# Another sequence for the dense jobs of the attention stage, and one set of rotation tiles

## The chip, the cores and the metric

The kernel runs on one core of a Trainium2 chip. The metric is the device time of one execution in microseconds (us). The sequences of TensorE (PE), VectorE (DVE), ScalarE (ACT), GpSimd (POOL) and SyncE (SP) run beside each other, each in its own order, and wait for each other through semaphores. All transfers between memory and the core are issued by SP here, one after the other.

## What is computed

One layer of an encoder over 1024 tokens of width 1024: a gated feed-forward block, a mixing block and a second gated feed-forward block, each with a residual. The change lies in the mixing block:

```python
proj = u @ w_in            # columns: qa, ka, va, xm, o_pre, ga, gb
ya = diff_attention(rope(qa), rope(ka), va)   # 8 heads, two score maps each, block-causal
yb = mlstm_branch(xm, o_pre)                  # 4 heads, conv, chunkwise scan
merged = sigmoid(ga) * (ya @ w_proj_a) + sigmoid(gb) * (yb @ w_proj_b)
h = h + gt2 * (merged @ w_out)
```

`rope` turns each pair (a, b) into (a cos - b sin, a sin + b cos).

## The kernel before

All matrix products are made of three float32r products of high and low parts (`mm3`), so each weight tile is fetched (512 KB, `wr`), cast on ACT into a high part (`wh`) and subtracted on DVE into a low part (`wl`). Two raw buffers (`raw`) and four pairs of high and low parts serve all of them.

The mixing block has two stages with chains of dependent small steps: the mLSTM (`stage_mlstm`) and the attention (`stage_attn`). The gaps that these leave on TensorE are filled with dense jobs, generators that emit a few matmuls at each step (`chunk` takes the next step of the first job in `self.jobs`). There are four kinds.

- `job_qk` (q, one for each head): four halves of 24 matmuls of 512 columns. The first two products are copied by ACT into the tiles `qa0` and `qa1` (one buffer each); the other two are each turned with one of these in `rotate`, which takes eight DVE steps and three ACT copies, writes the rotation tiles `ro` and stores four tiles of 256 KB to memory (`qkh`, `qkl`). The attention stage loads a head's keys and queries from there.
- `job_v` (v, one for two heads): eight tiles of 24 matmuls of 256 columns, each split by ACT and DVE, stored in pairs (`vh`, `vl`).
- `job_g` (g): gate columns, one weight unit and two halves of 24 matmuls for each tile of 128 columns.
- `job_b`: products of the mLSTM output, at the end of the list.

The order of the jobs is a string in `tile_block`: one q, four v, three q, then gates and q in turn. The planner's own times are 21.8 us of TensorE for a q, 21.7 for a v, 10.9 for a g of one tile and 5.45 for a b.

In the mLSTM stage a job is taken whenever the due time of the next mLSTM item lies ahead (`paced`); the order on ACT, DVE and SP is then left to the scheduler of the framework. The attention stage is laid out by a planner of the kernel itself, `Flow`. It simulates TensorE, ACT and DVE with a list of costs, and writes the instructions of all engines out in the order in which they come up in that model. A chain yields steps: "A" and "D" are operations of ACT and DVE with a cost, "P" matmuls, "X" a transfer, "take" and "give" a token that stands for a buffer, "need" and "set" a flag, "wait" a delay that stands for a transfer. When no matmul of the attention is ready, the planner calls `chunk`. The tokens are `raw`, `dn` (two PSUM banks for dense jobs), `rb` and `rot` (rotation), `qa0`, `qa1`, and those of the attention. A weight fetch is given 7 us (`lead`), the last store of a rotation 6.0 us. Jobs are begun up to three ahead, as long as they have no more than four weight units together (`begin_jobs`); a job begun outside the planner has its weights loaded at once, and a q then only the first of two.

Of the kernel before, what the change touches and what calls it, by code (L numbers as in the profile page):

```python
# [54 lines left out]
class Flow:  # L55
# [71 lines left out]
    def run(self):  # L127
        while self.live:
            while self.heap and self.heap[0][0] <= self.now:
                t, _, what = heapq.heappop(self.heap)  # L130
                if not isinstance(what, tuple):
                    self.advance(t, what)
                elif what[1] == "P":
                    self.pe.append(what)
                else:
                    gen, eng, cost, fn = what
                    fn()
                    self.free[eng] = max(self.free[eng], t) + cost
                    self.push(self.free[eng] + self.LAT, gen)
            if self.pe:  # L140
                gen, _, cost, fn = self.pe.pop(0)
                fn()
                self.now += cost
                self.push(self.now + self.LAT, gen)
                continue
            c = self.chunk()
            if c:
                self.now += c
            elif self.heap:
                self.now = max(self.now, self.heap[0][0])  # L150
            else:
                assert not self.live

class Net:
# [901 lines left out]
    def job_v(self, hp):  # L1056
# [10 lines left out]
        def keep(tt):  # L1067
            if tt % 2:
                for x, d in zip(vo, self.vd[hp]):
                    nc.sync.dma_start(out=d[:, :, tt - 1:tt + 1], in_=x)  # L1070

        for tt in range(8):
# [28 lines left out]
    def job_qk(self, hd):  # L1101
# [9 lines left out]
        def first(ps, n):  # L1111
            ab.append([None, [("give", f"qa{n}")] if self.flow else []])
            return [("take", f"qa{n}")] * len(ab[n][1]) + [("A", 0.6, lambda: keep(ps, n))]

        for i in range(2):
            while not w[i][2]:
                yield 0.0
            for n in range(NH):
                yield from self.proj_half(w[i], "qp", n, lambda ps, n=n: first(ps, n) if i == 0
                                          else self.rotate(hd, n, *ab[n], ps))  # L1120
                if len(w) == 1:
                    w.append(self.unit_ahead(self.a["win"][2 * hd + 1]))

    def rotate(self, hd, n, a, done, ps):
        nc, v, ns = self.nc, self.nc.vector, slice(n * NW, n * NW + NW)
# [7 lines left out]
        def to_b():  # L1133
            t["b"] = self.t512()
            nc.scalar.copy(t["b"], ps)

        def to_x():
            for c in "xyw":
                t[c] = self.rope.tile([P, NW], F32, name=self.nm("ro"), tag="ro", bufs=6)
            v.tensor_mul(t["x"], a, cos)  # L1140

# [3 lines left out]
                 ("D", 0.69, lambda: v.tensor_sub(t["x"], t["x"], t["y"])),  # L1145
                 ("D", 0.69, lambda: v.tensor_mul(a, a, sin)),
                 ("A", 0.62, lambda: nc.scalar.copy(t["y"].bitcast(F32R), t["x"])),
                 ("D", 0.69, lambda: v.tensor_mul(t["b"], t["b"], cos)),
                 ("D", 0.69, lambda: v.tensor_add(a, a, t["b"])),
                 ("D", 0.69, lambda: v.tensor_sub(t["x"].bitcast(F32R), t["x"], t["y"])),  # L1150
                 ("X", lambda: store(t["x"], t["y"], 0)),
                 ("A", 0.62, lambda: nc.scalar.copy(t["w"].bitcast(F32R), a)),
                 ("D", 0.69, lambda: v.tensor_sub(a.bitcast(F32R), a, t["w"])),
                 ("X", lambda: (store(a, t["w"], 1), self.turned(hd, n)))]
        if self.flow is None:
            return [x for x in steps if len(x) > 2 or x[0] == "X"]
        return [("take", "rb")] + steps[:8] + [("give", "rb")] + steps[8:] + [("wait", 6.0), ("give", "rot")] + done

    def turned(self, hd, n):

        self.heads_in.add(("qk in", hd, n))
        if self.flow is not None:
            self.flow.set(("qk in", hd, n))

# [27 lines left out]
    def load_y(self, n, src):  # L1192
        nc = self.nc
        ns = slice(n * NW, n * NW + NW)
        if n not in self.y:
            self.y[n] = [[self.u_tile(c, k, n) for c in "hl"] for k in range(KT)]
        done = []
        for k in range(KT):
# [4 lines left out]
            else:  # L1203
                def chain(k=k, hi=hi, lo=lo):
                    yield "wait", 5.0 + 0.7 * k
                    yield "A", 0.62, lambda: nc.scalar.copy(hi, lo.bitcast(F32))
                    yield "D", 0.69, lambda: nc.vector.tensor_sub(lo, lo.bitcast(F32), hi.bitcast(F32))
                    if k == KT - 1:
                        done.append(1)
# [3 lines left out]
    def job_b(self, n, m):  # L1213
# [4 lines left out]
        while not self.loaded[n]:  # L1218
# [4 lines left out]
        ps, free = yield from self.bank("ab")  # L1223
        evict = (("D", 0.7, lambda: nc.vector.tensor_mul(t, t, ps)), *free,
                 ("X", lambda: nc.sync.dma_start(out=self.bd[m][:, ns], in_=t)))

        for k in range(KT):
            ks = slice(k * P, k * P + P)
            if k == 4:
                self.defer(0.5, ("A", 0.63, lambda: nc.scalar.activation(t, t, AF.Exp, scale=-1.0)))  # L1230
            self.mm3(ps, (w[0][:, ks], w[1][:, ks]), [x for x in self.y[n][k]], k == 0, k == KT - 1)
# [21 lines left out]
    def chunk(self):  # L1253

        while self.jobs:
            self.begin_job(0) if self.flow is None else self.begin_jobs()
# [229 lines left out]
    def stage_attn(self, dense):  # L1486
        nc, tc = self.nc, self.tc
        nlam, gcol = self.lam[:, 2:3], self.lam[:, 3:4]
        with tc.tile_pool(name="a1", bufs=1) as a1, tc.tile_pool(name="a2", bufs=2) as a2, \
# [5 lines left out]
            qs, kh, kl = (a1.tile([P, 2, T], F32R, name=self.nm(c), tag=c) for c in ("Q", "Kh", "Kl"))  # L1495
            flow = Flow(lambda: self.chunk() if len(self.jobs) > KT or ("scored", 7, 3) in flow.flags else 0.0,
                        {"raw": 2, "dn": 2, "rb": 1, "rot": 2, "qa0": 1, "qa1": 1, "sc": 2, "pt": 1, "po": 1, "ah": 2, "p0": self.p0, "p1": 2, "osb": 1})

# [37 lines left out]
            def score(hd, j, i, c, a):  # L1536
# [45 lines left out]
                if (i, c) == (1, 1):  # L1582
                    yield "set", ("scored", hd, j)
                yield "D", 0.27 + 1.04e-3 * W, top
                yield "take", f"p{c}"
# [130 lines left out]
            for x in self.heads_in:  # L1716
                flow.set(x)
            self.begin_jobs()
            with tc.manual_schedule(engines={PE, ACT, DVE, SP}):
                self.flow = flow  # L1720
                flow.run()
                self.flow = None
# [45 lines left out]
def tile_block(ctx, tc, aps, dbg=()):  # L1768
# [57 lines left out]
    with ExitStack() as net.outer:  # L1826
        with ExitStack() as gst:
            net.stage_in(gst)
            net.set_lnexp(net.last_sig)
            order = "qvvvvqqqggqggqggqggqggggggg"  # L1830
            src = {"q": [[net.job_qk(hd), 2, None] for hd in range(8)], "v": [[net.job_v(hp), 2, None] for hp in range(4)],
                   "g": [[net.job_g(s, *j), len(j), None] for s, j in [(1, (j,)) for j in range(KT)]
                         + [(0, (j,)) for j in range(KT - 2)] + [(0, (KT - 2, KT - 1))]]}
            net.jobs = [src[c].pop(0) for c in order] + [[net.job_b(n, m), 1, None] for n in range(NH) for m in range(KT)]
            net.y, net.loaded, net.heads_in = {}, {}, set()
            net.left = 4 * 21.7 + 8 * 21.8 + 16 * 10.9 + 16 * 5.45
# [83 lines left out]
```

## Time and profile before

| | us |
|---|---|
| median of 3 runs | 2676.37 |
| their range | 2676.04 to 2682.2 |
| the profiled execution | 2680.27 |
| its span, first to last instruction | 2678.6 |

The profile is of one execution. Its page gives the busy time of each engine; the trace behind it can be asked for stretches of time, for waits and what ended them, for the chain of work that ended last, and for a list of instructions in order. All times within it are counted from the start of the span. The granted clock is a share of the full 2.4 GHz; 0.50 is the lower level, 1.2 GHz, and a figure between is a mean over the stretch. The mixing block's mLSTM stage lies between about 884 and 1203 us, the attention stage between 1203 and about 1840 us.

### The profile page before, as it was taken

The numbers are of one execution on the slowest core, as the hardware profiler recorded it, in microseconds if no ns is written. First come the engines' busy times: TensorE is split into PE (matmuls) and PEld (weight loads), VectorE is DVE, ScalarE is ACT, GpSimd is POOL, SyncE is SP. The second block draws the span as 40 slices with busy tenths as digits, with TensorE's granted clock in tenths as the row PEclk, the third lists the DMA queues.
The fourth block names the chain that finished last, engine by engine and source line by source line (L and its number), as shares of the span: only waits on it lengthen the run. The fifth ranks groups of instructions, "written<-read, shape, count | busy, mean of one in ns | idle before, by whom it ended". The sixth has DMA issues, their size and how long they took to land.

```text
span 2678.6 us, 35281 instructions
## 1 busy us (share of the span) xinstructions
PE 2590.4 (97%) x12704; PEld 2162.5 (81%) x12704; DVE 1789.2 (67%) x3214; ACT 1269.8 (47%) x2374; POOL 22.5 (1%) x85
## 2 busy tenths in 40 slices
PE   6999999999999999998899999999999999999998
PEld 4888888778878789996688888787888888888886
DVE  8977677778786456545666665574557766666967
ACT  6433333446444356653466664664345433334443
POOL 0000000000000000000000000000000000000000
PEclk8999999999999999998899999999999999999999
DMA  7434345733687645334444444557442333236433
GB/s 268 162 121 147 123 142 194 268 99 108 220 316 268 199 156 160 123 113 134 143 156 149 160 138 141 182 195 277 164 141 82 114 106 107 96 105 225 152 95 122
DMA packets 214791, 426.64 MB, mean 159 GB/s; under 512 B 21860, under 2 KB 83752, under 8 KB 214616
## 3 DMA queue, kind: packets, MB, share of 16 engines
q1 hardware_dynamic: 214616, 424.39, 47.1%
q8 instruction: 100, 1.64, 0.2%
q14 instruction: 75, 0.61, 0.1%
HBM read 301.24 MB, written 123.06 MB: 158 GB/s over the span
## 4 chain that ended last, share of the span: by engine, by line
PE 86%; DMA 5%; DVE 4%; ACT 2%; issue 1%; SPq 1%; POOL 0%; DVEq 0%; ACTq 0%; POOLq 0%
PE gu L264 10%; PE gu L266 10%; PE gu L265 10%; PE acc L264 5%; PE acc L265 5%; PE acc L266 5%; PE dn L264 2%; PE dn L266 2%; PE dn L265 2%; PE gp L264 2%; PE gp L266 2%; PE gp L265 2%; PE ab L264 2%; PE ab L266 2%; PE ab L265 2%; PE qp L264 2%
## 5 line engine op out<-in xcount | busy, mean ns | idle before, releaser
L264 PE MATMUL gu<-uh,wh 128*128 128x512 f32 x800 | 314.5, 393 | 10.9 <-ACT uh L333 8.8
L265 PE MATMUL gu<-ul,wh 128*128 128x512 f32 x800 | 314.0, 392 | 1.6 <-DVE ul L334 1.6
L266 PE MATMUL gu<-uh,wl 128*128 128x512 f32 x800 | 313.6, 392 | 0.0
L264 PE MATMUL acc<-uh,wh 128*128 128x512 f32 x616 | 241.5, 392 | 0.0
L265 PE MATMUL acc<-ul,wh 128*128 128x512 f32 x616 | 240.1, 390 | 0.5 <-DVE ul L270 0.5
L266 PE MATMUL acc<-uh,wl 128*128 128x512 f32 x616 | 239.7, 389 | 0.0
L269 ACT CAST wh<-wr 128x512 fp32r<-128x512 f32 x228 | 134.0, 619 | 204.2 <-PE gu L265 121.2
L264 PEld LDWEIGHTS gu<-uh,wh 128*128 128x128 f32 x800 | 151.4, 189 | 46.0 <-ACT uh L333 10.4
L265 PEld LDWEIGHTS gu<-ul,wh 128*128 128x128 f32 x800 | 151.5, 189 | 34.1 <-DVE ul L334 2.4
L266 PEld LDWEIGHTS gu<-uh,wl 128*128 128x128 f32 x800 | 151.6, 189 | 32.2 <-DVE wl L231 0.8
L264 PE MATMUL gu<-ut,wh 128*128 128x512 f32 x456 | 177.4, 389 | 0.0
L265 PE MATMUL gu<-ut,wh 128*128 128x512 f32 x456 | 177.4, 389 | 0.0
L266 PE MATMUL gu<-ut,wl 128*128 128x512 f32 x456 | 177.4, 389 | 0.0
L270 DVE TENSOR_TENSOR wl<-wr,wh 128x512 fp32r<-128x512 f32 x228 | 153.5, 685 | 0.1
L269 ACT CAST uh<-hr 128x512 fp32r<-128x512 f32 x154 | 95.3, 619 | 99.6 <-PE acc L266 74.1
L1563 ACT ACTIVATE p<-sc,lr 128x256 f32<-128x256 f32 (+7 forms) x128 | 95.1, 743 | 95.7 <-DVE lr L1558 82.0
L230 ACT CAST wh<-wr 128x1024 fp32r<-128x1024 f32 x75 | 78.7, 1049 | 126.9 <-PE wo L265 45.0
L264 PEld LDWEIGHTS acc<-uh,wh 128*128 128x128 f32 x616 | 115.6, 188 | 26.2 <-issue 2.2
L265 PEld LDWEIGHTS acc<-ul,wh 128*128 128x128 f32 x616 | 115.6, 188 | 25.5 <-DVE ul L270 1.3
L266 PEld LDWEIGHTS acc<-uh,wl 128*128 128x128 f32 x616 | 115.6, 188 | 24.0
L549 ACT COPY t<-gu 128x512 f32<-128x512 f32 x114 | 66.8, 586 | 136.5 <-PE gu L266 132.7
L219 DVE SCALAR_TENSOR_TENSOR ada<-ada,crep 128x1024 f32<-128x1024 f32 x72 | 87.6, 1220 | 60.4 <-DMA ada<-wada 60.2
(332 smaller groups left out, 6588.2 us busy)
## 6 DMA issues: line engine op xcount, KB each, us to landing
ada<-wada SPq DMA_DIRECT2D x72, 512.0 KB
wr<-win SPq DMA_DIRECT2D x48, 512.0 KB
wr<-w1gu SPq DMA_DIRECT2D x44, 512.0 KB
wr<-w2gu SPq DMA_DIRECT2D x44, 512.0 KB
wr<-wab SPq DMA_DIRECT2D x32, 512.0 KB
qkh<-ro SPq DMA_DIRECT2D x32, 256.0 KB
Kh<-qkh SPq DMA_DIRECT2D x64, 128.0 KB
Kl<-qkl SPq DMA_DIRECT2D x64, 128.0 KB
```

The costliest lines, as they stand in the source:

```text
L219: nc.vector.scalar_tensor_tensor(raw, raw, 1.0, self.crep, op0=ALU.mult, op1=ALU.mult, accum_out=self.mod[g][:, k:k + 1])
L230: nc.scalar.copy(hi, raw)
L264: mm(ps, w[0], x[0], start=start, stop=False, skip_group_check=again)
L265: mm(ps, w[0], x[1], start=False, stop=False, skip_group_check=again)
L266: mm(ps, w[1], x[0], start=False, stop=stop, skip_group_check=again)
L269: (eng or self.nc.scalar).copy(hi, src)
L270: self.nc.vector.tensor_sub(lo, src, hi.bitcast(F32))
L549: nc.scalar.copy(t, ps)
L1563: nc.scalar.activation(a[i][c][:, 0:W], x["ps"][:, 0:W], AF.Exp, bias=lr[:, 2 + c:3 + c], accum_out=lr[:, c:c + 1])
```

## The change

The list of jobs gets another sequence. Outside the planner, in the mLSTM stage, three q and two v are reached instead of one q and four v; in the attention stage two gate jobs or more stand between two q, and the last two v stand among them. A head's values are loaded only when their v has been stored (`arrived`, flag "v in").

A rotation uses one set of three `ro` tiles instead of two sets, with one token `rot` instead of two, and a buffer of its own (`rb`) for the product that it turns. `rb` is given back one step later, `qa0` and `qa1` 4 us later. The copy of the first product sets a flag, which the rotation needs.

The planner now puts an operation back until its engine is free in the model, where it used to write it out when it was ready and add the time to that engine's queue. Three conditions are written out that followed from the order before: the gate of a `job_b`, all parts of a loaded y, and the stop of the dense jobs when eight are left (`spare`).

```diff
                     gen, eng, cost, fn = what
+                    if self.free[eng] > t:
+                        self.push(self.free[eng], what)
+                        continue
                     fn()
-                    self.free[eng] = max(self.free[eng], t) + cost
+                    self.free[eng] = t + cost
...
+            if tt == 7:
+                self.arrived("v in", hp)
...
-            return [("take", f"qa{n}")] * len(ab[n][1]) + [("A", 0.6, lambda: keep(ps, n))]
+            return [("take", f"qa{n}")] * len(ab[n][1]) + [("A", 0.6, lambda: keep(ps, n)), ("set", ("kept", hd, n))]
...
         def to_b():
-            t["b"] = self.t512()
+            t["b"] = self.rope.tile([P, NW], F32, name=self.nm("rb"), tag="rb")
...
-                t[c] = self.rope.tile([P, NW], F32, name=self.nm("ro"), tag="ro", bufs=6)
-            v.tensor_mul(t["x"], a, cos)
+                t[c] = self.rope.tile([P, NW], F32, name=self.nm("ro"), tag="ro", bufs=3)
+            t["a"] = kept[0]
+            v.tensor_mul(t["x"], t["a"], cos)
...
-        return [("take", "rb")] + steps[:8] + [("give", "rb")] + steps[8:] + [("wait", 6.0), ("give", "rot")] + done
+        return ([("need", ("kept", hd, n))] if kept[1] else []) + [("take", "rb")] + steps[:9] + [("give", "rb")] + steps[9:] + [("wait", 6.0), ("give", "rot")] + [("wait", 4.0)] + kept[1]
...
-                    if k == KT - 1:
+                    parts.append(k)
+                    if len(parts) == KT:
                         done.append(1)
...
-        evict = (("D", 0.7, lambda: nc.vector.tensor_mul(t, t, ps)), *free,
+        evict = (("need", ("gate", n, m)), ("D", 0.7, lambda: nc.vector.tensor_mul(t, t, ps)), *free,
...
-        while self.jobs:
+        while len(self.jobs) > self.spare:
...
-            flow = Flow(lambda: self.chunk() if len(self.jobs) > KT or ("scored", 7, 3) in flow.flags else 0.0,
-                        {"raw": 2, "dn": 2, "rb": 1, "rot": 2, "qa0": 1, "qa1": 1, "sc": 2, "pt": 1, "po": 1, "ah": 2, "p0": self.p0, "p1": 2, "osb": 1})
+            flow = Flow(self.chunk, {"raw": 2, "dn": 2, "rb": 1, "rot": 1, "qa0": 1, "qa1": 1, "sc": 2, "pt": 1, "po": 1, "ah": 2, "p0": self.p0, "p1": 2, "osb": 1})
...
             def loads_v(hd):
+                yield "need", ("v in", hd // 2)
                 yield "need", ("valued", hd - 1)
...
-            order = "qvvvvqqqggqggqggqggqggggggg"
+            order = "qvqqvggqggvqggqggvqggqggggg"
```

## Rows read from the trace of the kernel before

**Rows 1.** The page, busy time and share of the span of each engine.
```profile
PE 2590.4 (97%) x12704; PEld 2162.5 (81%) x12704; DVE 1789.2 (67%) x3214; ACT 1269.8 (47%) x2374; POOL 22.5 (1%) x85
```

**Rows 2.** Stretches: length, busy PE, PEld, DVE, ACT, POOL, granted clock, DMA.
```profile
884.00:960.00 76.00, 64.79 (x414) 59.04 (x415) 33.80 (x70) 30.17 (x71) 1.69 (x4) 0.96 0.60 194
960.00:1140.00 180.00, 175.18 (x1415) 169.69 (x1414) 107.94 (x302) 110.30 (x340) 9.90 (x22) 1.00 0.45 147
...
1203.00:1240.00 37.00, 24.04 (x88) 17.62 (x87) 12.80 (x31) 10.54 (x25) 0.70 (x4) 0.72 0.70 200
...
1280.00:1340.00 60.00, 47.61 (x216) 38.78 (x215) 34.55 (x71) 25.38 (x53) 0.41 (x2) 0.86 0.47 155
1340.00:1600.00 260.00, 260.00 (x1364) 220.39 (x1363) 174.31 (x341) 161.07 (x310) 3.30 (x16) 1.00 0.44 148
1600.00:1760.00 160.00, 152.33 (x762) 126.75 (x761) 89.90 (x178) 90.71 (x175) 1.65 (x8) 0.98 0.53 176
```

**Rows 3.** Waits of PE, 1205 to 1830: us in total, times, longest.
```profile
PE qp L264 <- ACT qa L1109: 12.4, 2, 7.6
PE sc L1551 <- ACT p L1572: 7.4, 1, 7.4
...
PE qp L264 <- ACT wh L255: 3.4, 1, 3.4
```

**Rows 4.** Chain that ended last, 1270 to 1335: start, us, what.
```profile
1294.25 7.20 DMA qkl<-qa
...
1306.76 12.28 DMA qkl<-qa
```

**Rows 5.** Order of time on SP, 1200 to 1245: start, us, issue.
```profile
1208.15 0.56 SPq L1436 DMA_DIRECT2D yb<-hT  x1
...
1211.52 0.91 SPq L253 DMA_DIRECT2D wr<-win  x2
...
1227.97 7.03 SPq L253 DMA_DIRECT2D wr<-win  x3
```

**Rows 6.** Order of time on ACT, 1195 to 1250, idle time before in brackets.
```profile
1218.11 1.04 ACT L255 CAST wh<-wr 128x1024 fp32r<-128x1024 f32 x1 [5.33 <-DMA wr<-win]
```

**Rows 7.** Short stretches around the holes, as rows 2.
```profile
1216.20:1223.90 7.70, 0.37 (x2) 0.00 (x0) 3.37 (x6) 4.00 (x8) 0.00 (x0) 0.68 1.07 311
1223.90:1229.60 5.70, 4.47 (x14) 3.05 (x14) 2.42 (x6) 1.26 (x3) 0.20 (x1) 0.50 1.10 229
...
1233.40:1239.50 6.10, 6.02 (x13) 4.30 (x14) 2.94 (x6) 2.22 (x6) 0.00 (x0) 0.50 0.23 86
1294.50:1302.10 7.60, 0.04 (x1) 0.00 (x0) 0.01 (x1) 0.63 (x2) 0.00 (x0) 0.70 0.55 190
1302.10:1307.00 4.90, 4.89 (x13) 3.93 (x14) 1.79 (x6) 1.79 (x6) 0.00 (x0) 0.50 0.60 161
1314.60:1319.70 5.10, 0.27 (x3) 0.07 (x1) 0.49 (x1) 0.64 (x2) 0.00 (x0) 0.83 0.22 83
1319.70:1325.00 5.30, 5.30 (x13) 4.11 (x14) 3.30 (x7) 2.12 (x5) 0.00 (x0) 0.52 0.00 0
```

**Rows 8.** One DVE step of a rotation and of a v: min/median/max ns.
```profile
L1140 DVE TENSOR_TENSOR ro<-qa,cos x14: 679/682/685, 1244.0 to 1589.1; 128x512 f32<-128x512 f32 x14
...
L270 DVE TENSOR_TENSOR t<-vp,t x32: 411/423/426, 943.6 to 1203.7; 128x256 fp32r<-128x256 f32 x32
```

**Rows 9.** Order of time on ACT in the mLSTM stage, 929 to 943.
```profile
940.45 1.04 ACT L230 CAST wh<-wr 128x1024 fp32r<-128x1024 f32 x1 [7.31 <-DMA wr<-wv]
```

**Rows 10.** The stretch around it, as rows 2.
```profile
920.00:960.00 40.00, 34.04 (x255) 32.88 (x254) 23.37 (x52) 18.25 (x46) 1.20 (x3) 0.96 0.46 151
```

**Rows 11.** PE by line, first of three products: busy us, mean ns, idle before.
```profile
L264 PE MATMUL gp<-uh,wh 128*128 128x512 f32 x256 | 104.2, 407 | 0.0
```

**Rows 12.** Matmuls of the scores: first and last start us.
```profile
L1551 PE MATMUL sc<-Kh,Q x192: 220/389/799, 1208.3 to 1790.8; 128*128 128x512 f32 x96, 128*128 128x128 f32 x32, 128*128 128x256 f32 x32, 128*128 128x384 f32 x32
```

**Rows 13.** Tile wr, 1203 to 1830: idle time ahead of its users, us, times.
```profile
  ACT wh L255: 26.5, 15
```

More of the change, by code (lines that the diff above doesn't have):

```diff
@@ L1119, in job_qk, with rotate @@
                 yield from self.proj_half(w[i], "qp", n, lambda ps, n=n: first(ps, n) if i == 0
-                                          else self.rotate(hd, n, *ab[n], ps))
+                                          else self.rotate(hd, n, ab[n], ps))
                 if len(w) == 1:
                     w.append(self.unit_ahead(self.a["win"][2 * hd + 1]))
-    def rotate(self, hd, n, a, done, ps):
+    def rotate(self, hd, n, kept, ps):
         nc, v, ns = self.nc, self.nc.vector, slice(n * NW, n * NW + NW)
@@ L1145, in rotate, with arrived @@
                  ("D", 0.69, lambda: v.tensor_sub(t["x"], t["x"], t["y"])),
-                 ("D", 0.69, lambda: v.tensor_mul(a, a, sin)),
+                 ("D", 0.69, lambda: v.tensor_mul(t["a"], t["a"], sin)),
                  ("A", 0.62, lambda: nc.scalar.copy(t["y"].bitcast(F32R), t["x"])),
                  ("D", 0.69, lambda: v.tensor_mul(t["b"], t["b"], cos)),
-                 ("D", 0.69, lambda: v.tensor_add(a, a, t["b"])),
+                 ("D", 0.69, lambda: v.tensor_add(t["a"], t["a"], t["b"])),
                  ("D", 0.69, lambda: v.tensor_sub(t["x"].bitcast(F32R), t["x"], t["y"])),
                  ("X", lambda: store(t["x"], t["y"], 0)),
-                 ("A", 0.62, lambda: nc.scalar.copy(t["w"].bitcast(F32R), a)),
-                 ("D", 0.69, lambda: v.tensor_sub(a.bitcast(F32R), a, t["w"])),
-                 ("X", lambda: (store(a, t["w"], 1), self.turned(hd, n)))]
+                 ("A", 0.62, lambda: nc.scalar.copy(t["w"].bitcast(F32R), t["a"])),
+                 ("D", 0.69, lambda: v.tensor_sub(t["a"].bitcast(F32R), t["a"], t["w"])),
+                 ("X", lambda: (store(t["a"], t["w"], 1), self.arrived("qk in", hd, n)))]
         if self.flow is None:
             return [x for x in steps if len(x) > 2 or x[0] == "X"]
-        return [("take", "rb")] + steps[:8] + [("give", "rb")] + steps[8:] + [("wait", 6.0), ("give", "rot")] + done
-    def turned(self, hd, n):
-        self.heads_in.add(("qk in", hd, n))
+        return ([("need", ("kept", hd, n))] if kept[1] else []) + [("take", "rb")] + steps[:9] + [("give", "rb")] + steps[9:] + [("wait", 6.0), ("give", "rot")] + [("wait", 4.0)] + kept[1]
+    def arrived(self, *what):
+        self.heads_in.add(what)
         if self.flow is not None:
-            self.flow.set(("qk in", hd, n))
+            self.flow.set(what)
     def job_g(self, s, *js):
@@ L1196, in load_y @@
             self.y[n] = [[self.u_tile(c, k, n) for c in "hl"] for k in range(KT)]
-        done = []
+        done, parts = [], []
         for k in range(KT):
@@ L1229, in job_b @@
             if k == 4:
-                self.defer(0.5, ("A", 0.63, lambda: nc.scalar.activation(t, t, AF.Exp, scale=-1.0)))
+                self.defer(0.5, ("A", 0.63, lambda: nc.scalar.activation(t, t, AF.Exp, scale=-1.0)),
+                           ("set", ("gate", n, m)))
             self.mm3(ps, (w[0][:, ks], w[1][:, ks]), [x for x in self.y[n][k]], k == 0, k == KT - 1)
@@ L1583, in score @@
                     yield "set", ("scored", hd, j)
+                    if (hd, j) == (7, 3):
+                        self.spare = 0
                 yield "D", 0.27 + 1.04e-3 * W, top
@@ L1718, in stage_attn @@
             self.begin_jobs()
+            self.spare = KT
             with tc.manual_schedule(engines={PE, ACT, DVE, SP}):
@@ L1834, in tile_block @@
             net.jobs = [src[c].pop(0) for c in order] + [[net.job_b(n, m), 1, None] for n in range(NH) for m in range(KT)]
-            net.y, net.loaded, net.heads_in = {}, {}, set()
+            net.y, net.loaded, net.heads_in, net.spare = {}, {}, set(), 0
             net.left = 4 * 21.7 + 8 * 21.8 + 16 * 10.9 + 16 * 5.45
```

## The prediction, made blind

> **What bounds the kernel now.** The page comes first. TensorE is busy for 2590.4 of 2678.6 us [rows 1], so a new order can win no more than the 88 us in which it is idle and what it loses at a lower clock. The question is how much of that lies where the diff acts. The table of stretches tells it [rows 2]: the mLSTM stage up to 1203 us, the attention stage from there to about 1840. In 884 to 960 TensorE idles 11.2 us (76.00 less 64.79), in 960 to 1140 4.8. In the attention stage it idles 13.0 us in 1203 to 1240 and 12.4 in 1280 to 1340, then nothing for 260 us, and 7.7 in 1600 to 1760. The two early holes also have a granted clock of 0.72 and 0.86, the later rows 0.98 to 1.00: the early holes cost more than their idle time. In the full stretch from 1340, DVE is busy 174 of 260 us and ACT 161. They have room on average, and hold TensorE up only where an order blocks.
>
> What ended the waits is in the table of waits [rows 3]: two waits of qp for the ACT copy into qa, 12.4 us together; one of sc for ACT, 7.4; one of qp for a weight cast, 3.4. The chain over the second hole [rows 4] names the cause of the first pair: a copy starts when a store of qa lands, 7.20 us after its issue at 1294.25, and the next one waits 12.28 us for another store. A query/key job keeps its first product in qa0 and qa1, turns it in place and stores it; the tiles are single. Jobs q1, q2 and q3 stand in a row, so the next job wants qa while the last one's store is on its way. The planner counts 6.0 us for that store.
>
> For the first hole, SP's issues [rows 5] and ACT's line [rows 6] are read side by side. SP comes to the last store of the mLSTM stage at 1208.15 and issues two weight fetches at 1211.52, which by the code are the two units of q2. Their casts stand in ACT's queue ahead of an exponential; ACT stands still for 5.33 us, and TensorE waits for the exponential. The second unit of q1, for which TensorE is next in line, is asked for only when a raw buffer comes back; its fetch stands behind the loads of head 0, at 1227.97, and is the 3.4 us wait.
>
> **Part 1, q jobs apart.** In the attention stage no q follows a q any more; two gate jobs (2 x 10.9 us by the planner) lie between. q1 and q2 are done in the mLSTM stage, where 108 us of dense work are spread over 319. The two qa waits go. Their price [rows 7]: idle 7.60 - 0.04 and 5.10 - 0.27, so 12.4 us; and the stretches behind them, 1302.1 to 1307 and 1319.7 to 1325, run at a granted 0.50 and 0.52, the lower of the two levels, so half of 4.9 + 5.3 is lost, 5.1 us. Gain 17.5 us. Bounds: 0 if another wait stands behind (next on ACT is the copy of the other half, into a tile that is free then); 17.5 at most.
>
> The Trainium skill, "DMA: Bandwidth & Descriptors", section "Anatomy of one DMA", fits a transfer to about 2.0 us plus its bytes by 436 GB/s, on another issue path; as an estimate that is 2.6 us for one of these 256 KB stores. By it the planner's 6.0 us would always do, no qa wait would exist and Part 1 would be worth nothing; the rows differ, with 7.20 and 12.28 us [rows 4], and the measurement decides.
>
> **Part 2, the start of the attention stage.** The mLSTM stage takes dense work until its own items run out: now one q and four v (21.8 + 4 x 21.7 by the planner), then three q and two v, the same to 0.2 us. So it ends in the same place, at the end of a v. Behind that stands q1 now, with one of two weights loaded; then two gate jobs with one each, both begun ahead of the attention stage and so early in SP's queue. The 3.4 us wait goes, and the second spell at half clock with it. What stays: q3 is begun at the moment at which q2 is begun now, so the fetches at 1211.52, ACT's stop and TensorE's first wait, 7.70 - 0.37 = 7.3 us [rows 7], stay. Behind a wait of that length the low clock lasted some 5 us in the other hole. TensorE was busy 4.47 + 6.02 us at 0.50 here, a loss of 5.2 us; 2.6 remain. Gain 3.4 + 2.6 = 6.0 us. Bounds: 0, and with the first wait gone too 6.0 + 7.3 + 2.6 = 15.9.
>
> **Part 3, what the mLSTM stage gets.** Two q take the place of two v. A q has two rotations of eight DVE steps at 682 ns, 10.9 us; a v has eight subtractions at 423 ns, 3.4 us [rows 8]. DVE gets 15 us more, in a stage where it is busy 108 of 180 us [rows 2]; ACT's copies and casts are eight against eight. That lies beside TensorE's work while the order holds. Stores are equal in number, eight of 256 KB in either kind of job, so SP's issues are only moved. With one set of rotation tiles instead of two, the second rotation of a job waits for the first one's stores; halves are some 16 us apart here (5.45 x 319 / 108). Lower bound 0. The upper bound is the one place where a rotation, its stores and a weight fetch meet in this stage now: a fetch holds ACT for 7.31 us [rows 9], and 920 to 960 loses 6.0 us idle and 1.6 by a clock of 0.96 (0.04 x 40), 7.6 us [rows 10]. Four such places (two jobs, two rotations) make 30. I take 4, about as much again as 960 to 1140 idles now, because the bad place stands in the crowd of loads at the start of the stage, where DMA runs at 0.60 against 0.45 later [rows 2].
>
> **Part 4, what the attention stage gets.** Two v run there, sixteen tiles of 24 matmuls, 2.7 us each by the planner, where a half of g is 5.45: a bank has to be emptied in half the time. TensorE never waited for the emptying of a g bank: 256 first matmuls, no idle before them [rows 11]. Lower bound 0; upper 16 x 0.3 = 5, a third of a us for each tile; I take 1. One rotation set: the planner starts a second rotation 6.0 us after the last store of the first; its first DVE step needs only the tile whose store is issued two operations earlier, so 7.3 us in fact. Against 7.20 us [rows 4] that costs nothing; against 12.28 it is 5 us in each of five jobs, 25 in all, with the scores' maxima queued behind it on DVE and TensorE behind those. I take 1, nearer to the first row, since the longer store belongs to the crowd of rotations that goes. Two q less and two v more also take 15 us off DVE here, worth nothing where TensorE is full.
>
> **Part 5, edits with one answer.** An operation is emitted when its engine is free in the planner, not when it is ready. Operations of an engine were already served in the order in which they became ready, and putting one back keeps that order, so no time in the planner moves. Only a v's subtraction, which rides on an ACT step, reaches DVE's queue later, and that can only spare DVE a wait. The added conditions (values in, gate ready, first product kept, all eight parts of y there) ask for what is done long before. The tightest is v2: it is through after 87 us of the 414 that the planner has for the attention stage's 637, so near 1340; head 4 needs it near 1500 (eight heads from 1208 to 1791 [rows 12], 73 us each). The stop at eight remaining jobs was there already. Together 0. The holes of 1600 to 1760 have the same work around them and stay, moved a little.
>
> **Sum.** -17.5 - 6.0 + 4 + 1 + 1 = -17.5 us. From the profiled run's 2680.27 that is 2662.8. That run lies 3.9 above the median of the runs shown; from the median, 2676.37, it is 2659.
>
> **Rivals.** A: the first wait goes too, because the gate jobs in hand let q3's casts come late enough. For: TensorE needs no new weight for 21.8 us of dense work. Against: the casts' place in ACT's queue is set by the planner's 7 us, which don't change. -15.9 in place of -6.0: 2649. B: the gain is spent again by late transfers. In the attention stage ACT stands 26.5 us before its weight casts, 15 times [rows 13]; most of that is covered, and another order can uncover four of them at the 3.4 us that one cost TensorE [rows 3]: 2659 + 13.6 = 2673. For: where a cast waits is chance, and the order of transfers changes everywhere. Against: 260 full us with the same traffic. C, slower: the rotations moved into the mLSTM stage block ACT and DVE at all four places. -23.5 + 2 + 30 = +8.5: 2685; it turns slower than before from the third place on (3 x 7.6 = 22.8 against 21.5). For: the one time that a rotation ran in that stage, it happened. Against: it was at the stage's crowded start.
>
> **How the numbers follow.** About 0.3% (8 us) is what a measurement tells from no change, so faster is under 2668, slower over 2684. Forecast (2649 to 2668) 0.62, A 0.12, B 0.18, C 0.08. Faster 0.74, same 0.18, slower 0.08. The range must take in most of A and B and much of what Part 3 can cost: 2643 to 2681.
>
> **What would show it.** Right: no wait of qp for qa in the attention stage; gp, not qp, behind the first scores; 1280 to 1340 full at a clock of 1.00; the 7 us wait of sc near 1217 still there. Wrong: new idle time in 960 to 1203 with ACT or DVE behind a ro tile or a weight (Part 3); vp waiting for its bank, or DVE for a ro store, in the attention stage (Part 4); the first wait gone (A).

## The result, and the profile after

The changed kernel takes 2698.22 us (median of four runs, 2690.48 to 2701.49) where the kernel before takes 2677.77: 1.007 times as long, interval 1.0044 to 1.0095. The prediction was 2659, so it missed the sign, and its range ended at 2681. Timed a second time (e13 below) the change gives 2696.11, ratio 1.0064 (1.0049 to 1.0079). The profiled run is the shortest of the first four, 2690.48 us with a span of 2688.8: against the profiled run of before, 2680.27, its trace can explain +10.2, and that of e13, 2695.14, +14.9.

TensorE's line of the page, to be held against [rows 1]:

```profile
PE 2597.3 (97%) x12704; PEld 2166.2 (81%) x12704; DVE 1788.1 (67%) x3214; ACT 1270.8 (47%) x2374; POOL 22.8 (1%) x85
```

The same number of instructions, and TensorE just as full by its busy share. The stretches, columns as [rows 2]:

```profile
884.00:960.00 76.00, 68.88 (x447) 63.30 (x448) 35.41 (x74) 31.92 (x76) 1.70 (x4) 0.96 0.63 202
960.00:1140.00 180.00, 170.93 (x1223) 158.13 (x1222) 111.90 (x302) 108.92 (x329) 9.25 (x22) 0.99 0.44 142
1203.00:1240.00 37.00, 29.00 (x154) 24.26 (x153) 11.68 (x30) 12.08 (x36) 0.49 (x3) 0.86 0.77 216
1280.00:1340.00 60.00, 57.53 (x362) 50.78 (x361) 37.82 (x78) 35.69 (x73) 0.62 (x3) 1.00 0.54 166
1340.00:1600.00 260.00, 250.39 (x1413) 215.72 (x1411) 162.56 (x319) 146.69 (x285) 3.09 (x15) 0.98 0.48 148
1600.00:1760.00 160.00, 150.53 (x724) 125.40 (x725) 93.46 (x184) 86.40 (x168) 1.44 (x7) 0.94 0.52 162
```

Both early holes have shrunk: 1203 to 1240 idles 8.0 us instead of 13.0, 1280 to 1340 2.5 instead of 12.4, at a clock of 1.00 instead of 0.86. But 960 to 1140 idles 9.1 instead of 4.8, and 1340 to 1600, which was full, idles 9.6. TensorE's waits, 1205 to 1830 (us in total, times, longest), name other causes than [rows 3]. (qp, vp and gp are the products of a q, a v and a gate job; sc is a score, p its exponential, pt the transposed p, ah and al the high and low part of that, po its product with the values.)

```profile
PE sc L1559 <- DMA Kh<-qkh: 11.8, 3, 6.0
PE sc L1559 <- ACT p L1571: 6.2, 3, 3.1
PE po L267 <- ACT ah L1628: 5.3, 1, 5.3
PE sc L1559 <- DMA Kl<-qkl: 2.0, 1, 2.0
```

No qp waits for qa any more. The scores now wait for the loads of their keys, which were no cause before. Where the attention stage begins and ends is read from the first matmul of the scores and the first that uses the output weights (tile views of sc and wo; instances, min/median/max ns, first and last start):

```profile
L1559 PE MATMUL sc<-Kh,Q x192: 220/389/799, 1217.3 to 1802.0; 128*128 128x512 f32 x96, 128*128 128x128 f32 x32, 128*128 128x256 f32 x32, 128*128 128x384 f32 x32
L267 PE MATMUL wo<-mg,wh x128: 387/389/799, 1904.2 to 2034.9; 128*128 128x512 f32 x128
```

Before, the scores began at 1208.3 [rows 12] and wo at 1894.1. So the stages up to the scores end 9.0 us later, and from the first score to wo it takes 686.9 us against 685.8: what the attention stage gained in front it lost behind.

The experiments are held together by one table. "Lost" is worked out from the list of TensorE's matmuls: the distance from each to the next, less the distance that its shape has at full clock; it counts idle time and low clock alike, and a stretch without loss can come out some tenths off 0. Columns are the median in us (runs), the start of the first score, the time from there to the first wo, and the lost us in four stretches.

| kernel | us | first score | to wo | 960–1200 | 1200–1260 | 1260–1340 | 1500–1700 |
|---|---|---|---|---|---|---|---|
| before | 2677.77 | 1208.3 | 685.8 | 10.3 | 19.8 | 17.6 | 5.1 |
| after | 2698.22 (4) | 1217.3 | 686.9 | 25.9 | 12.1 | 2.9 | 21.5 |
| e13 after again | 2696.11 (4) | 1218.3 | 690.6 | 26.5 | 10.6 | 4.0 | 22.8 |
| e8 after again | 2689.98 (1) | 1218.7 | 685.1 | 25.9 | 10.7 | 3.5 | 19.8 |
| e1 after, two sets | 2670.45 (7) | 1211.9 | 672.4 | 17.2 | 11.0 | 4.6 | 4.5 |
| e4 after, five ro tiles | 2688.43 (6) | 1215.8 | 684.8 | 20.7 | 10.9 | 3.9 | 18.9 |
| e2 before, one set | 2678.94 (10) | 1198.7 | 692.6 | 11.3 | 17.2 | 23.4 | 0.3 |
| e7 before, q apart | 2667.55 (5) | 1206.5 | 672.4 | 10.1 | 19.8 | 0.0 | 4.4 |
| e3 after, v ahead | 2659.33 (4) | 1203.9 | 668.0 | 12.0 | 17.1 | 0.2 | 1.0 |
| e5 = e3, two sets | 2667.78 (4) | 1208.8 | 675.3 | 11.0 | 20.4 | -0.1 | 8.6 |
| e6 = e3, five ro tiles | 2661.59 (4) | 1209.5 | 665.7 | 10.7 | 18.5 | 0.1 | 1.3 |
| e9 after, head 6's stores moved | 2683.69 (10) | 1221.4 | 677.4 | 24.1 | 13.9 | 3.6 | 10.8 |
| e12 heads 6 and 7 | 2685.70 (7) | 1220.0 | 681.1 | 25.2 | 13.5 | 3.8 | 14.3 |
| e10 = e3, a g first | 2678.85 (10) | 1211.3 | 683.8 | 9.7 | 16.3 | 7.8 | 1.5 |
| e11 = e10, later casts | 2678.66 (10) | 1209.3 | 685.0 | 11.0 | 13.9 | 5.9 | 2.2 |
| e14 = e3, stores at the keys | 2696.86 (4) | 1207.9 | 702.4 | 9.8 | 18.7 | -0.1 | 20.1 |

Kernels with the same work up to the first score differ there by some 4 us (e3 and e14, after and e9), so a difference of that size in this column says nothing.

Over 880 to 1900 the lost time is 82.4 us before, 91.7 after (+9.3, of +10.2 between the profiled runs) and 97.9 in e13 (+15.5, of +14.9): the whole difference lies in these stages. The medians differ by more, 20.5 us, because each trace is of one execution: that of before lies 2.5 us above its median, that of after 7.7 us below its own.

Two readings of the new losses come from the trace of after itself. First, the mLSTM stage, in the chain that ended last (start, us, what):

```profile
1074.12 0.62 ACT ro L1153
1074.77 6.17 DMA qkh<-ro
1080.97 0.69 DVE ro L1146
```

and in DVE's order of time (idle before it in brackets):

```profile
1080.97 0.69 DVE L1146 TENSOR_TENSOR ro<-qa,cos 128x512 f32<-128x512 f32 x1 [2.70 <-DMA qkh<-ro]
1081.58 0.42 DVE L273 TENSOR_TENSOR scl<-w,sch 128x256 fp32r<-128x256 f32 x1
1081.91 0.41 DVE L273 TENSOR_TENSOR mq<-qkp,mq 128x256 fp32r<-128x256 f32 x1
```

The second rotation's first step writes the tile that the first rotation's store still reads. DVE, which takes its instructions in order, stands 2.70 us for it, and the mLSTM's scl and mq behind it come late: the next qkp matmul starts at 1082.38, after a wait of 3.1 us for mq. A second such wait of DVE, 3.14 us, ends at 1162.43, and TensorE then waits 2.0 us for scl. Before had no wait of TensorE for either. The rotations come so close because the first step of the second one reads the kept product and not its own half, whose matmuls still run at 1084.

Second, the hole at 1588 to 1600. SP's order of time (start, us, issue):

```profile
1573.76 2.30 SPq L1136 DMA_DIRECT2D qkh<-ro  x1
1576.16 0.82 SPq L1136 DMA_DIRECT2D qkl<-qa  x1
1577.03 1.43 SPq L1512 DMA_DIRECT2D Q<-qkh  x1
1578.51 1.79 SPq L1512 DMA_DIRECT2D Q<-qkl  x1
1580.35 0.78 SPq L1517 DMA_DIRECT2D Kh<-qkh  x1
1581.17 0.71 SPq L1517 DMA_DIRECT2D Kl<-qkl  x1
1581.93 0.61 SPq L1517 DMA_DIRECT2D Kh<-qkh  x1
1582.58 0.60 SPq L1517 DMA_DIRECT2D Kl<-qkl  x1
1585.92 0.57 SPq L1512 DMA_DIRECT2D Q<-qkh  x1
1588.49 0.57 SPq L1512 DMA_DIRECT2D Q<-qkl  x1
...
1591.75 0.59 SPq L256 DMA_DIRECT2D wr<-win  x1
```

By the trace's instruction list the transfers of SP use eight completion semaphores in turn, and an issue waits for the last transfer on its semaphore, the one eight places ahead of it, whatever that is. The rows show it: SP stops at 1585.92 and 1588.49, eight places behind the two stores of head 6's second rotation, and SP's waits there are put down to them:

```profile
SPq L1512 <- DMA qkh<-ro: 2.7, 1, 2.7
SPq L1512 <- DMA qkl<-qa: 2.0, 1, 2.0
```

These are loads of head 5, which has nothing to do with head 6's stores. The chain shows what that does (start, us, what), and ACT's order of time how long it stands for the fetch:

```profile
1577.03 12.05 DMA Q<-qkh
...
1591.75 4.82 DMA wr<-win
```

```profile
1596.59 1.04 ACT L258 CAST wh<-wr 128x1024 fp32r<-128x1024 f32 x1 [12.39 <-DMA wr<-win]
...
1598.47 0.59 ACT L1628 CAST ah<-pt 128x512 fp32r<-128x512 f32 x1
```

The weight fetch behind the loads is issued at 1591.75, its cast stands on ACT ahead of the ah copy, and TensorE's po waits 5.3 us for ah, the third line of its waits above.

The waits of the scores have another reason, since the key loads that end them were issued ahead of SP's stops. The one that ends at 1590.39 is for a load issued at 1581.93, landed 8.3 us later; the one that ends at 1659.95 is for a load issued right behind head 7's stores (chain):

```profile
1651.97 7.89 DMA Kh<-qkh
```

By the semaphore events of this trace the first keys of heads 2, 3, 4 and 7, which have no rotation stores just ahead, land 2.8 to 3.9 us after their issue; those of heads 1 and 6, which have, take 6.7 to 8.7 us. The planner gives a head's first keys 4.5 us. So stores cost twice: the loads behind them land late, and the issues eight places behind them stand.

### The profile page after: what moved, and what is told of

It reads as the page before. It is cut to its first block, busy times and chain, and to the rows that moved or that the text cites. A ratio compares the mean times of both kernels' runs of the same rounds, so it can differ in the third digit from the quotient of the medians.

```text
span 2688.8 us, 35271 instructions
## 1 busy us (share of the span) xinstructions
PE 2597.3 (97%) x12704; PEld 2166.2 (81%) x12704; DVE 1788.1 (67%) x3214; ACT 1270.8 (47%) x2374; POOL 22.8 (1%) x85
## 4 chain that ended last, share of the span: by engine, by line
PE 84%; DMA 6%; DVE 4%; ACT 3%; SPq 1%; issue 1%; POOL 0%; DVEq 0%; ACTq 0%; POOLq 0%
PE gu L267 10%; PE gu L268 10%; PE gu L269 10%; PE acc L267 5%; PE acc L268 5%; PE acc L269 5%; PE dn L267 2%; PE dn L268 2%; PE dn L269 2%; PE ab L269 2%; PE ab L267 2%; PE ab L268 2%; PE gp L267 2%; PE gp L268 2%; PE gp L269 2%; PE qp L267 2%
## 5 line engine op out<-in xcount | busy, mean ns | idle before, releaser
L267 PE MATMUL gu<-uh,wh 128*128 128x512 f32 x800 | 314.6, 393 | 10.7 <-ACT uh L336 8.8
```

Source lines behind the costliest of these rows:

```text
L267: mm(ps, w[0], x[0], start=start, stop=False, skip_group_check=again)
```

## The experiments

Two questions were open: is it the single set of rotation tiles or the sequence, and if the set, is it the tile (DVE waits for a store) or the planner's token (stores issued elsewhere)? All ratios are against the kernel before.

**e1: the change with two sets.** Six ro tiles and two tokens; for room, b comes from the pool that it used before.

```diff
-            t["b"] = self.rope.tile([P, NW], F32, name=self.nm("rb"), tag="rb")
+            t["b"] = self.t512()
...
-                t[c] = self.rope.tile([P, NW], F32, name=self.nm("ro"), tag="ro", bufs=3)
+                t[c] = self.rope.tile([P, NW], F32, name=self.nm("ro"), tag="ro", bufs=6)
...
-... "rot": 1, ...
+... "rot": 2, ...
```

> The changed kernel with two sets of rotation tiles again (six ro tiles, token rot 2, the turned product in a t512 tile as before); its job sequence and its planner stay. Theory M: in the mLSTM stage of the changed kernel DVE stands before the first step of a second rotation until the store of the first one lands (twice some 6 us at 1074.77 and 1156.30, once 7.6 at 919.13), and that delays the stage. Then this kernel's mLSTM stage ends some 8 us earlier than the changed one's (first score matmul near 1212 rather than 1220), and the time is some 8 us under the changed kernel's 2698: 2690. Rival: it is the 15 us of extra DVE work of two more q jobs, whatever the tiles. Then the stage ends as late as in the changed kernel and the time stays within 3 us of 2698.

2670.45 us, ratio 0.9972 (0.996 to 0.9984). That is 20 us under what was expected: both losses come back, where only the first was in the expectation. Some 27 us come back by the medians, 20.0 by the profiled runs: 5.4 ahead of the first score and 14.5 from there to wo. The stretches (columns as above):

```profile
960.00:1140.00 180.00, 174.17 (x1260) 161.32 (x1258) 113.74 (x306) 111.69 (x336) 9.25 (x22) 1.00 0.45 146
...
1340.00:1600.00 260.00, 256.85 (x1434) 220.64 (x1433) 165.17 (x327) 152.24 (x296) 3.09 (x15) 1.00 0.45 148
```

The DVE wait near 1081 and the hole at 1588 are both gone. The single set is what makes the change slower, in this sequence.

**e2: the kernel before with one set.**

```diff
-... name=self.nm("ro"), tag="ro", bufs=6)
+... name=self.nm("ro"), tag="ro", bufs=3)
...
-... "rot": 2, ...
+... "rot": 1, ...
```

> The kernel before with one set of rotation tiles (three ro tiles, token rot 1) and nothing else. Theory M: only the one q job that runs in the mLSTM stage is hit there (+2 to +4 us); in the attention stage the planner counts the single set and q jobs stand in a row, so the holes at 1220 to 1340 grow by some 5 us: 2677 + 8 = 2685. Rival (the planner hides a single set): within 3 us of 2677.

2678.94, ratio 1.0007 (0.9998 to 1.0016): no difference, so the rival came and not the 2685. The hole at the row of q jobs grows (17.6 to 23.4), others shrink. The single set alone costs nothing on balance; it takes the new sequence.

**e3: the change with v ahead again.** The q jobs stay apart, but all values are done in the mLSTM stage.

```diff
-            order = "qvqqvggqggvqggqggvqggqggggg"
+            order = "qvvvvqggqggqggqggqggqggqggg"
```

> The changed kernel with the sequence qvvvvqggqggqggqggqggqggqggg: all four v and one q in the mLSTM stage as before the change, the other seven q two gate jobs apart in the attention stage; one rotation set and the new planner stay. Theory M together with theory V (the holes that the changed kernel has after 1520 come from the v jobs in the attention stage and the later q): the mLSTM stage ends as before the change, the two waits for qa are gone, 2677 - 17 = 2660, and no hole over 3 us stands between 1340 and 1700. Rival T (late transfers show up somewhere whatever the sequence, because the attention stage now runs ahead of its key loads): the holes after 1340 come to 10 to 20 us again, 2672 to 2680.

2659.33, ratio 0.993 (0.9915 to 0.9945): the fastest of all kernels here, with one set. Both new losses are gone:

```profile
960.00:1140.00 180.00, 174.61 (x1410) 169.15 (x1409) 108.85 (x304) 109.05 (x337) 9.90 (x22) 1.00 0.45 146
...
1340.00:1600.00 260.00, 258.95 (x1352) 218.44 (x1351) 173.38 (x340) 156.08 (x303) 3.29 (x16) 1.00 0.47 155
```

**e7: the kernel before with that sequence.** One line: `order = "qvvvvqggqggqggqggqggqggqggg"` in place of `"qvvvvqqqggqggqggqggqggggggg"`.

> The kernel before with that same sequence and nothing else: two rotation sets, old way of emitting. If the gain is the sequence alone: as e3_v_ahead, within 4 us (2656 to 2664). If one set and the new planner are what costs in the attention stage: some 8 us under e3_v_ahead.

2667.55, ratio 0.9959 (0.9944 to 0.9975): 8 us above e3, where the same time or 8 us less had been expected. Setting the q apart, alone, is worth 10 us; the lost time in 1260 to 1340 goes from 17.6 to 0.0, which is Part 1's mechanism and its size, but 1700 to 1900 loses 17.0 instead of 13.1.

**e5 and e6: e3 with two sets (as in e1), and e3 with five ro tiles but one token.**

> The kernel of e3_v_ahead (all v and one q ahead, one set, new planner: 2659.3) with two sets again (six ro tiles, token 2, product in a t512 tile). It differs from e7_before_q_apart (2667.6) in the planner alone. If the new way of emitting brought the 8 us between those two: near 2659. If the single set brought them: near 2667.

> The kernel of e3_v_ahead (2659.3) with five ro tiles instead of three. Only one second rotation runs in the mLSTM stage there, at its start; theory M gives 0 to -3 us: 2656 to 2660. If theory R is right for this sequence too: some 2 us less again.

e5: 2667.78, ratio 0.9955 (0.994 to 0.997); e6: 2661.59, ratio 0.9936 (0.992 to 0.9953), within the noise of e3 and not below it as expected. e5 and e7 have the same sequence and two sets and differ in the planner's other edits alone: 2667.78 and 2667.55. So emission, flags and added conditions cost nothing in this sequence, as Part 5 said. In this sequence a second token makes the kernel 8 us slower, not faster. e5's trace loses 8.6 us in 1500 to 1700 and e3's 1.0: there po waits 5.4 us for ACT (osq), and ACT has stood 9.70 us for a weight fetch (cast at 1671.05), and that fetch is issued at 1658.12, right behind two rotation stores. That looks like the hole at 1588 again; it is read from the trace, and no run tried it by an edit.

**e4: the change with five ro tiles, one token.** The second rotation finds free tiles; where the planner puts its operations and stores is unchanged.

```diff
-... name=self.nm("ro"), tag="ro", bufs=3)
+... name=self.nm("ro"), tag="ro", bufs=5)
```

> The changed kernel with five ro tiles in place of three and nothing else: token rot stays 1, so the planner's order is that of the changed kernel, but a second rotation finds free tiles for its first two results. Theory M (DVE stands behind the store of the first rotation in the mLSTM stage): the stage loses some 6 us less than in the changed kernel, as with two sets. For the holes that the changed kernel has after 1500 (21.5 us in its profile, 4.5 with two sets) there are two theories. Theory R: in the attention stage too a second rotation waits for tiles in fact; then the holes go and the time is near that of two sets, 2671. Theory O: one token makes the planner place the second rotation some 20 us later, so that its stores stand on SP in the middle of a head's loads; then the holes stay, 2685 to 2692.

2688.43, ratio 1.0038 (1.0026 to 1.005). The mLSTM stage gets 5.2 us of lost time back (25.9 to 20.7); DVE has no wait for a store there, and TensorE's waits at 1082 and 1164 are gone, though one of 2.6 us for mq comes at 1173. The late holes stay, in the same places. TensorE's waits, 1500 to 1700, after and then e4:

```profile
PE sc L1559 <- DMA Kh<-qkh: 5.8, 2, 3.8
PE po L267 <- ACT ah L1628: 5.3, 1, 5.3
```

```profile
PE sc L1559 <- DMA Kh<-qkh: 6.8, 2, 4.2
PE po L267 <- ACT ah L1628: 5.1, 1, 5.1
```

So the tile costs time in the mLSTM stage; in the attention stage it is the token, that is, where the stores are issued.

**e9 and e12: the change with the stores of head 6's second rotation (e12: of heads 6 and 7) issued behind head 5's last loads (e12: behind those of the head ahead).** What stands behind the first store in a rotation moves with it: one ACT copy, one DVE subtraction, and the return of rot and of qa. The order of the rest is left to the planner as before.

```diff
+        if (hd, n) == (6, 1):
+            steps.insert(next(i for i, x in enumerate(steps) if x[0] == "X"), ("need", ("qk", 5, 3)))
```

> The changed kernel with one thing moved: the four stores of head 6's second rotation, which stand on SP between the first and the second group of head 5's key loads (1572 to 1577), are issued behind all of head 5's loads. Theory O (these stores in the middle of the loads hold SP, whose issue waits for the transfer eight places ahead of it, so that the next weight fetch and with it ACT and TensorE are late): the hole at 1588 to 1600 (some 12 us with its spell at the lower clock) goes, those at 1522 and 1656 stay, and the time is 8 to 12 us under the changed kernel's 2690 to 2698: 2680 to 2688. Rival: the fetch is late because 24 key loads stand ahead of it in any case; then the hole stays and so does the time.

> As e9_s6_behind, and the four stores of head 7's second rotation, which stand right ahead of head 6's first key loads (1645 to 1650), also go behind those loads. Theory O: the wait of the scores for the key load at 1656 (4 us and its clock) goes as well, another 4 to 7 us: 2675 to 2683. Rival: as e9_s6_behind within 2 us.

e9: 2683.69, ratio 1.0016 (1.0007 to 1.0025), 12 to 15 us less than the change by the medians; between the profiled runs it is 5.5 (2685.01 against 2690.48), 9.5 less from the first score to wo and 4.1 more ahead of it, where the edit changes nothing. The hole at 1588 to 1600 is gone, and the waits over 1.4 us in 1500 to 1700 are down to

```profile
PE sc L1561 <- DMA Kh<-qkh: 4.1, 1, 4.1
```

which is the hole near 1650, where head 7's stores stand. e12: 2685.70 (1.0029, 1.0018 to 1.004): that hole goes as well, but one of 6.3 us appears from 1678 to 1685, and nothing more is won, where 2675 to 2683 had been expected. In the new hole TensorE waits for ACT (osq), and ACT has stood 11.09 us for a weight fetch (cast at 1681.98) that was issued at 1672.77, behind head 7's stores in their new place.

**e14: stores put ahead of loads in the fast kernel.** e3, with the second rotation's stores of heads 2 to 7 held until the head ahead has its last scores, which is where the next loads of keys are issued. As in e9, the last ACT copy and DVE subtraction of the rotation and the return of its tokens are held with them.

```diff
+        if n == 1 and hd > 1:
+            steps.insert(next(i for i, x in enumerate(steps) if x[0] == "X"), ("need", ("scored", hd - 1, 3)))
```

> The kernel of e3_v_ahead (2659.3, no hole over 1.3 us between 1300 and 1700) with the four stores of each second rotation of heads 2 to 7 held back until the last scores of the head before are placed, so that they stand on SP directly ahead of the next head's loads; all else as it was. Theory O: the scores then wait for their keys at six places, 4 us and some lower clock each, 20 to 35 us: 2680 to 2695. Rival (four stores, 2.2 us of issue, are hidden by the 4.5 us that the planner gives a key load): 2659 to 2664.

2696.86, ratio 1.0063 (1.0044 to 1.0081): 37.5 us slower than e3 by the move of 24 stores and what goes with them. TensorE's waits from 1240 to 1840, e14 and then e3:

```profile
PE sc L1561 <- DMA Kh<-qkh: 25.8, 6, 9.0
```

```profile
PE sc L1559 <- DMA Kh<-qkh: 0.7, 1, 0.7
```

Six heads, six waits. SP's order in e14 at the first of them:

```profile
1350.77 0.51 SPq L1136 DMA_DIRECT2D qkl<-qa  x1
...
1355.29 0.60 SPq L1519 DMA_DIRECT2D Kh<-qkh  x1
...
1356.58 0.61 SPq L1514 DMA_DIRECT2D Q<-qkh  x1
1359.94 0.57 SPq L1514 DMA_DIRECT2D Q<-qkl  x1
```

The issue at 1359.94 is the eighth behind the store of 1350.77 and stands 2.7 us for it, as in after. But the score that waits until 1361.95 waits for the load of 1355.29, ahead of that stop, which lands 6.6 us after its issue. In all six places the load that ends the wait takes 5.6 to 7.7 us; in e3 the first keys of the same heads take 2.7 to 3.6. And the loads are issued 4.6 to 9.0 us behind the last score of the head ahead, where e3 issues them at once: a head's loads are placed behind its own last stores, which stand late here. In after the stores in the way belong to a later head, so this part is not in the change. e14 shows the late landing behind stores; its 37.5 us are not the price of that alone.

**e10 and e11: e3 with a gate job ahead of the second q, to clear the first wait; e11 holds the first casts 8 us longer in the planner as well.**

```diff
-            order = "qvvvvqggqggqggqggqggqggqggg"
+            order = "qvvvvgqggqggqggqggqggqggqgg"
...
-            yield "wait", self.lead
+            yield "wait", self.lead + (8.0 if self.flow.now < 5.0 else 0.0)
```

> The kernel of e3_v_ahead (2659.3) with a gate job ahead of the first q in the attention stage: sequence qvvvvgqggqggqggqggqggqggqgg. The second step of the prediction by itself: the fetch of the first q's second unit is no longer what TensorE needs next. By it the 3.6 us wait near 1225 and half of the lower clock behind it go, -6 us: 2653. The first wait (7.5 us near 1211) stays. Rival: the later q of every head come closer to their loads, and what is won at 1225 is lost between 1400 and 1700: 2659 or more.

> As e10_g_first, and a weight fetch begun in the first 5 us of the attention stage is given 15 us by the planner instead of 7, so that its cast stands later in ACT's queue. If the 7.5 us wait of the scores near 1211 is ACT standing before that cast (rows 6 of the kernel before), the wait goes, with the lower clock behind it: -8 to -10 us against e10_g_first, 2644. If it is the scores' own chain or the load of the keys: no change against e10_g_first.

2678.85 (0.9993, 0.9982 to 1.0004) and 2678.66 (0.9994, 0.9985 to 1.0003): all of e3's gain is gone, where 2653 and 2644 had been expected; the rival of each came. The lost time in 1260 to 1500, nothing in e3, is 16.8 and 20.3 us, and the waits are again those of sc for key loads (in e11 21.2 us in four places from 1205 to 1460, the first wait among them). With every q one gate job later, its stores meet the loads of a head: in both traces rotation stores stand within 9 us ahead of the first keys of heads 1, 2 and 3, which take 5.3 to 8.0 us to land. And the first wait stays in e11, where the first casts are held back. Its chain (start, us, what):

```profile
1208.77 2.46 DMA yb<-hT
...
1212.14 6.82 DMA wr<-win
...
1218.97 5.58 DMA Kh<-qkh
```

SP can load the keys only when the mLSTM stage's last stores are issued, and the load takes its own 5.58 us. The cast of [rows 6] was the last to come, but the key load is as late: in the trace of before the load for those scores, issued at 1218.10, lands at 1223.69, and the score starts at 1223.93.

**e8 and e13: the change again, to see that its holes and its time are its own.**

> The changed kernel once more, for a second profile. If the holes after 1500 belong to its order of instructions, they stand in the same places again, 15 to 25 us together. If they were chance in one execution, they come to under 8 us or stand elsewhere.

> The changed kernel timed again. If its first median (2698) stands for it: 2694 to 2700. If its profiled executions (2690) stand for it: 2687 to 2693.

Both show the first score, the lost time of the four stretches and the holes of after within 1 to 2 us (table); e8 is a single run.

## Why the prediction was wrong, point by point

**Part 1 (-17.5) was right.** The two waits of qp for qa are gone, and 1260 to 1340 loses 2.9 us instead of 17.6, a gain of 14.7; e7, which does this alone, gains all 17.6 there.

**Part 2 (-6.0) was right in size, and partly in mechanism.** 1200 to 1260 loses 7.7 us less, gp stands behind the first scores, and a wait of 6.0 us stays among them, so rival A didn't come. But that wait is now put down to the key load; the chain of after over it:

```profile
1217.77 2.46 DMA yb<-hT
...
1221.13 6.60 DMA wr<-win
...
1227.75 5.59 DMA Kh<-qkh
```

and e11, in another sequence, shows the same wait with the casts held back.

**Part 3 (+4, upper bound 30) was mis-sized.** By first scores it is +9.0; in lost time 960 to 1200 gives +15.6 and 884 to 960 gives back 3.8, together 11.8. The mechanism was among those named, DVE behind a rotation's store. I put it at the crowded start, where DVE does wait 4.2 us for one (at 926.83), and it came in mid-stage too, 5.8 us in two places. That "halves are some 16 us apart here" was the wrong premise: the first step of a rotation does not need its half, so it came before the store's 6.17 us were over. Of the 15.6, five tiles give back 5.2 (e4) and two sets 8.7 (e1). What is left even with two sets, 17.2 against e7's 10.1, some 7 us, goes with two q in place of two v; how it is made up isn't settled.

**Part 4 is the step that failed.** "Against 7.20 us [rows 4] that costs nothing" asked only whether the tile is free when the second rotation starts. It looked at DVE, and DVE has no wait for a store of ro in the attention stage. (The reason given for the 1, that the store of 12.28 us belongs to a crowd that goes, was wrong too: by the semaphore events of after the rotation stores of that stage still take 5.7 to 13.6 us from issue to landing.) What the one token moves is the second rotation's four stores, to a later place in SP's queue, and the prediction did not ask what they then stand ahead of. They stand ahead of loads of head 5 and a weight fetch, and of the keys of head 6; 1500 to 1700 loses 16.4 us more, against 1 forecast for the single set. Shown by e4 (free tiles, holes stay), e1 (second token, holes gone) and e9 (four stores moved, one hole gone); e14 shows that loads right behind stores land late. That two v run in this stage (+1) can't be told apart from it by these runs, but between 1205 and 1830 the matmuls of vp waited 1.6 us in all for a subtraction.

**That the holes of 1600 to 1760 stay fell for the same reason.** The stretch idles 9.5 us instead of 7.7, at a clock of 0.94 instead of 0.98: the claim was argued from the work around them, and the order of transfers around them had changed.

**Part 5 (0) was right, as far as tried:** e5 and e7 differ by 0.2 us. Undoing the emission edit alone in the changed kernel wasn't tried.

**The rivals were no alternatives.** B (late transfers, 13.6) and C (blocked in the mLSTM stage, 30) have causes that don't exclude each other. Both came, C with 11.8 of its 30 and B with 16.4 for its 13.6: by the lost time -14.7 - 7.7 + 11.8 + 16.4 and 3.6 in 1700 to 1900 make +9.4. The prediction gave B and C a chance each, and none to both at once, and so its range ended short. Both at their full price would have been 2659 + 13.6 + 26 (the 30 less the 4 in the sum) = 2699; that this lies next to the measured median is chance, since neither came at its price. B came only in part as told: of its causes one weight cast was late, the other waits were for keys.

**Open:** what the change's runs differ by (2690 to 2701; e13's trace loses 6.2 us more than that of after, spread over all stretches), what e12 and e5 would win without the late fetch that their traces show, how the 16.4 us divide between late landings and stopped issues, and the 7 us of two q in the mLSTM stage.

## What to carry to other kernels

When an edit changes a token, a buffer count or a sequence, ask of each transfer that it moves which queue it goes through, what then stands behind it and how late that lands; whether its tile is free is only half the question. Before you give chances to rivals, ask if they exclude each other, and let the range hold the case in which both come. If a change has two halves, try each alone: here q apart with the values left where they were (e3) takes 18 us off (ratio 0.993), and with the values and the first q jobs moved among each other the same edits add 20.

## What the runs showed of the hardware that was not expected

A transfer of SP was held up by one that it has nothing to do with: with eight completion semaphores in turn, an issue stood 2.0 to 2.7 us for a store eight places ahead. Key loads of 128 KB right behind rotation stores landed 6.7 to 8.7 us after their issue in after (heads 1 and 6) and 5.6 to 8.7 in e14, where those of heads 2 to 7 in e3 took 2.7 to 3.6. The 256 KB stores took 6.17 us from issue to landing in mid-mLSTM and about 12 us among the loads (from 1573.76 to the issue that waited for it at 1585.92). The Trainium skill, "DMA: Bandwidth & Descriptors", section "Anatomy of one DMA", has a fit for transfers issued by GpSimd that would give 2.6 us for these stores as an estimate. These rows, of transfers issued by SP beside others, differ, and the measurement decides.
